# A diffusion layer's token-mixing heads with TensorE held to a written order

## The chip, the cores and the metric

One core of one Trainium2 chip runs the whole layer as one program. Its engines work in parallel, each on its own queue of instructions, and meet at semaphores: PE (TensorE, matrix products), DVE (VectorE), ACT (ScalarE), POOL (GpSimd) and SP, which issues DMAs. The metric is the device time of one execution in microseconds (us), as the median of several runs; one further execution was profiled.

## The reference

The layer has two parts. Token mixing computes eight heads over 256 context and 1024 latent tokens, four with an mLSTM memory and four with retention, each scanned in both directions in chunks of 128 tokens. Then a router lets each of 16 experts choose 128 tokens. Cut to what matters:

```python
def step(carry, inp):                      # mLSTM, one chunk, one direction
    ...
    s = jnp.einsum('bhtk,bhsk->bhts', qc, kc) * d_w
    num = jnp.einsum('bhts,bhsv->bhtv', s, vc) + i_w[..., None] * jnp.einsum('bhvk,bhtk->bhtv', C, qc)
    h = num / jnp.maximum(jnp.abs(den), jnp.exp(-m_t))[..., None]
    ...
y_m = jax.nn.sigmoid(parts[3]) * head_rmsnorm(m_sum, mlstm_norm_w)   # gate, norm per head
y_r = jax.nn.silu(parts[8]) * head_rmsnorm(r_sum, ret_norm_w)
y = jnp.concatenate([y_m, y_r], axis=-1) @ w_out
...
xl = xl + g2 * expert_choice_ffn(...)      # 16 experts, SwiGLU of width 2816
```

## The kernel before

The program has stages: adaLN and normalization of the inputs (to about 45 us), the heads, the output projection with the router, and the experts, which take two thirds of the time.

The heads run in the order 4, 0, 1, 2, 3, 5, 6, 7 (`HEADS`; 0 to 3 are mLSTM, 4 to 7 retention), called places 0 to 7 here. A head works through ten blocks of 128 tokens, two of context and eight latent ones. `gemm` (line 371) multiplies a block's normalized input with the head's 512 weight columns (gate, q, k, v): 24 products of 512 columns into the PSUM tile `g`, in eight steps of three, since inputs and weights are split in a high and a low part. A context block needs 256 columns only. `prep` (line 516) takes `g` apart: `v`, a gate `th` and `o`, and `qk` (with a rotary step for retention), transposes q and k (PSUM tile `T`, lines 570 and 571, copies `kT` and `qT`), forms the masked product `S` into `k1` or `k2`, and the state update `U` from `kw` and `v`, which a scan over the blocks takes into `st`.

`outp` (line 632) belongs to the head before: for one of its blocks the products `O` and `I` (for retention both in one tile) give the unnormalized rows; then `it`, `dn`, `hb`, `hs` divide and sum the two directions, `sq` and `rsqrt_mean` (lines 130 and 131, on POOL) give the norm `r`, line 674 multiplies to `z`, line 676 transposes `z` on TensorE, and a copy `zt` is stored. It is called after `prep` at the first eight blocks of the next head.

Weights of the next head come by `load_w`, four tiles `raw` of 512 KB, each split by ACT (`whi`, line 194) and DVE (`wlo`, line 195). The pool keeps eleven `whi` and eleven `wlo`, eight of the present head and three of the next. `ada2` (line 691) multiplies 512 KB of the adaLN matrix with a row, on DVE (line 694), at every second block. It shares the two buffers named `raw` with the weights.

Nothing fixes the order of TensorE in the heads: a scheduler puts each engine's instructions in an order by its own estimate of times. Each engine's queue is then worked in that order. An engine wrapped in `Ordered` (lines 138 to 144) keeps the order in which the code calls it; it is used before the heads only.

Of the kernel before, what the change touches and what calls it, by code (L numbers as in the profile page):

```python
# [8 lines left out]
F32 = mybir.dt.float32  # L9
# [12 lines left out]
NT = T // 128  # L22
# [98 lines left out]
def build(tc, A, out):  # L121
# [246 lines left out]

    pg_cur = [None]

    def gemm(wc, tt):
        his, los = wc
        c0 = 256 if tt < NTC else 0
        if tt != 1:
            pg_cur[0] = pg.tile([128, 512], F32, name="g")
        p = pg_cur[0]
        dst = p[:, 256 * tt:256 * tt + 256] if c0 else p
        hh, hl = htile(tt)
        for k in range(KD):
            for q, (a, w) in enumerate(((hh, his[k]), (hh, los[k]), (hl, his[k]))):  # L380
                PE.matmul(dst, lhsT=a[:, k], rhs=w[:, c0:512],  # L381
                          start=(k == 0 and q == 0), stop=(k == 7 and q == 2))
        return dst
# [132 lines left out]
    def prep(h, tt, p):  # L516
# [2 lines left out]
        lat = tt >= NTC  # L519
        NV = 130 if mls else 128  # L520
        r0, r1 = (row_of(0, tt, h), row_of(1, tt, h)) if mls else (0, 0)
        v = mp.tile([128, 130], F32, name="v", bufs=11)
        S.copy(v[:, 0:128], p[:, -128:])
        if mls:
            G.memset(v[:, 128:129], 1.0)
# [2 lines left out]
        if lat:  # L528
            th = mp.tile([128, 128], F32, name="th")
            S.activation(th, p[:, 0:128], AF.Tanh, scale=0.5)  # L530
            o = mp.tile([128, 128], F32, name="o", bufs=10)
            if mls:
                G.tensor_scalar(th, th, 0.5, 0.5, op0=ALU.mult, op1=ALU.add)
                G.tensor_tensor(o, th, d["nw"], op=ALU.mult)
            else:
                V.scalar_tensor_tensor(th, th, 1.0, p[:, 0:128], op0=ALU.add, op1=ALU.mult)
                G.tensor_scalar(th, th, 0.5, 1.0, op0=ALU.mult, op1=ALU.mult)
                G.tensor_tensor(o, th, d["nw"], op=ALU.mult)
            d["o"][tt] = o
# [23 lines left out]
        for dr in range(2):  # L563
            wcol = ct[:, 3, (r0, r1)[dr]:(r0, r1)[dr] + 1] if mls else d["kw"][:, dr:dr + 1]
            if tt == (NTT - 1, NTC)[dr]:
                continue
            G.tensor_scalar(kw[:, dr], qk[:, 1], wcol, QK, op0=ALU.mult, op1=ALU.mult)
        if lat:
            pt = ps.tile([128, 2, 128], F32, name="T", bufs=2)
            PE.transpose(pt[:, 0], qk[:, 0], ident)  # L570
            PE.transpose(pt[:, 1], qk[:, 1], ident)
            kT = mp.tile([128, 128], F32, name="kT")
            S.copy(kT, pt[:, 1])
            qT = mp.tile([128, 128], F32, name="k2", bufs=10) if mls else mp.tile([128, 128], F32, name="qTt")
            V.tensor_copy(qT, pt[:, 0])
            if not mls:
                qE = mp.tile([128, 2, 128], F32, name="k1", bufs=10)
                V.tensor_tensor(qE, pt[:, 0:1].broadcast_to([128, 2, 128]), d["e2"], op=ALU.mult)
                d["k1"][tt] = qE
            pS = psu.tile([128, 1, 128], F32, name="S")  # L580
            PE.matmul(pS[:, 0], lhsT=kT, rhs=qT, start=True, stop=True)
            if mls:
                mb = mp.tile([128, 2, 128], F32, name="t1")
                G.tensor_tensor(mb, aux, mbig, op=ALU.add)
                for dr in range(2):
                    r_ = (r0, r1)[dr]
                    S.activation(mb[:, dr], mb[:, dr], AF.Exp, bias=ct[:, 0, r_:r_ + 1], scale=-1.0)
                P = mp.tile([128, 2, 128], F32, name="k1", bufs=10)
                V.scalar_tensor_tensor(P, pS.broadcast_to([128, 2, 128]), QK, mb, op0=ALU.mult, op1=ALU.mult)
                d["k1"][tt], d["k2"][tt] = P, qT  # L590
            else:
                P = mp.tile([128, 128], F32, name="k2", bufs=10)
                V.scalar_tensor_tensor(P, pS[:, 0], QK, d["dm"], op0=ALU.mult, op1=ALU.mult)
                d["k2"][tt] = P
# [26 lines left out]
        else:  # L621
            if tt < NTT - 1:
                V.scalar_tensor_tensor(st(tt + 1)[:, 0], st(tt)[:, 0], decay(0), pU[:, 0], op0=ALU.mult, op1=ALU.add)
            if tt > NTC:
                if tt < NTT - 1:
                    S.copy(st(tt - 1)[:, 1], pU[:, 1])
                else:
                    V.scalar_tensor_tensor(st(tt - 1)[:, 1], st(tt)[:, 1], decay(1), pU[:, 1],
                                           op0=ALU.mult, op1=ALU.add)
        d["kt"][tt] = decay(1)  # L630

    def outp(h, tt, store=True):
        d = hd[h]
        mls = h < 4
        st = d["st"]
        if NTC < tt < NTT - 1:
            V.scalar_tensor_tensor(st[tt - 1][:, 1], st[tt][:, 1], d["kt"][tt], st[tt - 1][:, 1],
                                   op0=ALU.mult, op1=ALU.add)
        v, o, k1, k2 = d["v"][tt], d["o"][tt], d["k1"][tt], d["k2"][tt]
        hs = mp.tile([128, 128], F32, name="hs", bufs=3)  # L640
        sq = mp.tile([128, 128], F32, name="sq")
        ss = mp.tile([128, 1], F32, name="ss", bufs=3)
        if mls:
            r0, r1 = row_of(0, tt, h), row_of(1, tt, h)
            pO = ps.tile([128, 2, 130], F32, name="O")
            for dr in range(2):
                PE.matmul(pO[:, dr], lhsT=k1[:, dr], rhs=v, start=True, stop=True)
            pI = ps.tile([128, 2, 130], F32, name="I")
            PE.matmul(pI, lhsT=k2, rhs=st[tt], start=True, stop=True)
            it = mp.tile([128, 2, 130], F32, name="it")  # L650
            for dr in range(2):
                r_ = (r0, r1)[dr]
                S.activation(it[:, dr], pI[:, dr], AF.Copy, scale=ct[:, 1, r_:r_ + 1])
            V.tensor_tensor(it, pO, it, op=ALU.add)
            dn = mp.tile([128, 2], F32, name="dn")
            den = it[:, :, 128]
            V.tensor_tensor(dn, den, ct[:, 2, r0:r1 + 1:r1 - r0], op=ALU.max)
            V.scalar_tensor_tensor(dn, den, -1.0, dn, op0=ALU.mult, op1=ALU.max)
            V.reciprocal(dn, dn)
            hb = mp.tile([128, 128], F32, name="hb")  # L660
            G.tensor_scalar(hb, it[:, 1, 0:128], dn[:, 1:2], 1.0, op0=ALU.mult, op1=ALU.mult)
            V.scalar_tensor_tensor(hs, it[:, 0, 0:128], dn[:, 0:1], hb, op0=ALU.mult, op1=ALU.add)
            S.activation(sq, hs, AF.Square, accum_out=ss)
        else:
            pO = ps.tile([128, 128], F32, name="OI"[tt % 2])
            PE.matmul(pO, lhsT=k2, rhs=v[:, 0:128], start=True, stop=False)
            PE.matmul(pO, lhsT=k1[:, 0], rhs=st[tt][:, 0], start=False, stop=False)
            PE.matmul(pO, lhsT=k1[:, 1], rhs=st[tt][:, 1], start=False, stop=True)
            V.tensor_copy(hs, pO)
            S.activation(sq, hs, AF.Square, accum_out=ss)  # L670
        r = mp.tile([128, 1], F32, name="r", bufs=3)
        rsqrt_mean(r, ss, DH, mp)
        z = mp.tile([128, 128], F32, name="z")
        V.scalar_tensor_tensor(z, hs, r, o, op0=ALU.mult, op1=ALU.mult)
        pz = ps.tile([128, 128], F32, name="T", bufs=2)
        PE.transpose(pz, z, ident)
        zt = mp.tile([128, 128], F32, name="zt", bufs=3)
        S.copy(zt, pz)
        c = tt - NTC
        if store:  # L680
            nc.sync.dma_start(zt_d[h, :, c * 128:(c + 1) * 128], zt)
        return zt
# [58 lines left out]
        zsplit(c, 0, zr)  # L741

    todo = list(range(32))
    for n, h in enumerate(HEADS):
        head_start(h)
        for i in range(NTT):
            pr = ExitStack()
            if n == 0 and i < 4:
                pr.enter_context(tc.high_priority(offset=300))
            if i == 0:  # L750
                ps01 = [gemm(wcur, j) for j in range(NTC)]
            p = gemm(wcur, i) if i >= NTC else ps01[i]
            if n == 0 and i == 3:
                gates()
            if i == (6 if n == 0 else 0) and n + 1 < H:
                wnext = load_w(HEADS[n + 1])
            prep(h, i, p)
            pr.close()
            if n and i < NT:
                outp(HEADS[n - 1], NTT - 1 - i)  # L760
            if n == 1 and i == 0:
                silu_row()
            if n and i % 2 and todo:
# [1 line left out]
            if n == H - 1 and i == 4:  # L765
                V.tensor_tensor(mcol, mcol, cols[:, 16:48], op=ALU.add)
                V.scalar_tensor_tensor(mcol[:, 16:24], mcol[:, 16:24], 1.0, cols[:, 56:64], op0=ALU.add, op1=ALU.mult)
                g1bc.append(cp.tile([128, D], F32, name="crow"))
                col2row(g1bc[0], 0, lambda half: ps.tile([128, 512], F32, name="T", bufs=2))
            if n == H - 1 and i in (4, 5):  # L770
                zfirst(NT + 3 - i)
            if n == H - 1 and 5 < i < NTT:
                split_wout(*load_wout(0, 2 * (i - 6)))
            if n == H - 1 and i == 3:
                wo1 = [load_wout(1, k, 1) for k in range(6)]
        wcur = wnext

    def ygemm(y, c, half, ks):
        zh, zl = zz[0][:, c % 2], zz[1][:, c % 2]
# [611 lines left out]
```

## Time and profile before

| | us |
|---|---|
| median of 3 runs | 2279.93 (2277.79 to 2281.03) |
| the profiled execution, its own time | 2278.13 |
| its span, first to last instruction | 2276.4 |
| heads with output work beside them | 132 to 598 |
| experts | 772 to the end |

The profile gives for each engine the time it was busy, for each stretch the clock that TensorE was granted (1.00 is 2.4 GHz, 0.50 is 1.2 GHz), and for each wait the instruction that ended it. Long products overlap in the record: each lasts 0.39 us but the next starts 0.23 us later, so that the distance of two starts is the time one costs. Weight loads (PEld) run beside the products.

### The profile page before, as it was taken

How to read it: one execution, taken by the hardware profiler on the slowest of the kernel's cores; microseconds unless marked ns; L12 is line 12 of the kernel's file. 1: busy time of each engine (PE TensorE's matmuls, PEld its weight loads, DVE VectorE, ACT ScalarE, POOL GpSimd, SP SyncE). 2: the span in 40 equal slices, each digit the busy share in tenths (PEclk: the TensorE clock that was granted, in tenths of full speed). 3: DMA queues.
4: the chain of work that ended last, by engine and by line, in shares of the span. 5: the costliest groups of instructions: out<-in, count | busy, mean ns of one | idle time of the engine just before them, and what ended most of it. 6: DMA issues, size and time to landing. Idle time of an engine off the chain costs nothing.

```text
span 2276.4 us, 31305 instructions
## 1 busy us (share of the span) xinstructions
PE 2218.7 (97%) x11334; PEld 1852.1 (81%) x11334; DVE 1792.6 (79%) x2162; ACT 1431.2 (63%) x1854; POOL 355.1 (16%) x716
## 2 busy tenths in 40 slices
PE   7999999999899999999999999999999999999997
PEld 4788888888787788888888888888888888888885
DVE  6454545655735999999898898998988989889887
ACT  6533444322433676777777777677777777777775
POOL 2344444444411000000000000000000000000015
PEclk9999999999999999999999999999999999999999
DMA  7223322334375799999999999999999999999995
GB/s 279 64 61 107 102 69 77 103 111 125 106 242 204 308 357 370 355 389 390 372 395 365 380 392 367 401 366 382 389 368 400 367 382 389 368 391 377 371 405 233
DMA packets 134576, 664.71 MB, mean 292 GB/s; under 512 B 14381, under 2 KB 44181, under 8 KB 66837
## 3 DMA queue, kind: packets, MB, share of 16 engines
q1 hardware_dynamic: 127221, 634.73, 72.7%
q0 software_dynamic: 6768, 24.83, 3.7%
q10 hardware_dynamic: 432, 3.15, 0.4%
q8 instruction: 89, 1.46, 0.3%
q14 instruction: 66, 0.54, 0.1%
HBM read 637.50 MB, written 25.15 MB: 291 GB/s over the span
## 4 chain that ended last, share of the span: by engine, by line
PE 80%; DMA 7%; DVE 6%; issue 2%; ACT 2%; POOL 2%; SPq 0%; POOLq 0%; DVEq 0%; ACTq 0%
PE w_gate L144 20%; PE w_up L144 20%; PE y L144 19%; PE g L381 11%; DMA raw<-in_wada 4%; PE T L144 3%; PE y L783 2%; DVE lo L144 2%; DMA raw<-in_win 1%; PE U L599 1%; POOL r L131 1%; DMA xt<-in_x 1%; DVE raw L694 1%; DMA zr<-zt_d 1%; POOL rs_m L130 1%
## 5 line engine op out<-in xcount | busy, mean ns | idle before, releaser
L144 DVE TENSOR_TENSOR lo<-raw,hi 128x2048 fp32r<-128x2048 f32 x528 | 1180.0, 2285 | 74.8 <-ACT hi L144 70.2
L144 ACT CAST hi<-raw 128x2048 fp32r<-128x2048 f32 x528 | 979.6, 1904 | 41.5 <-PE w_up L144 38.6
L144 PE MATMUL w_gate<-hi,xh 128*128 128x512 f32 (+1 forms) x768 | 294.0, 383 | 0.7 <-ACT xh L144 0.7
L144 PE MATMUL w_gate<-hi,xl 128*128 128x512 f32 (+1 forms) x768 | 286.4, 373 | 0.0
L144 PE MATMUL w_up<-lo,xh 128*128 128x512 f32 (+1 forms) x768 | 285.4, 372 | 1.0 <-DVE lo L144 1.0
L144 PE MATMUL w_up<-hi,xh 128*128 128x512 f32 (+1 forms) x768 | 285.9, 372 | 0.0
L144 PE MATMUL w_gate<-lo,xh 128*128 128x512 f32 (+1 forms) x768 | 285.8, 372 | 0.0
L144 PE MATMUL w_up<-hi,xl 128*128 128x512 f32 (+1 forms) x768 | 285.3, 371 | 0.0
L144 ACT CAST th<-T 128x512 fp32r<-128x512 f32 x96 | 53.0, 552 | 340.7 <-PE T L144 340.7
L381 PE MATMUL g<-whi,hh 128*128 128x512 f32 (+1 forms) x640 | 246.6, 385 | 1.3 <-ACT qk L561 1.2
L381 PE MATMUL g<-whi,hl 128*128 128x512 f32 (+1 forms) x640 | 244.3, 382 | 1.0 <-DVE hl L361 1.0
L381 PE MATMUL g<-wlo,hh 128*128 128x512 f32 (+1 forms) x640 | 242.9, 380 | 0.0
L144 PE MATMUL y<-lo,th 128*128 128x512 f32 x704 | 222.3, 390 | 1.3 <-DVE lo L144 1.3
L144 PE MATMUL y<-hi,th 128*128 128x512 f32 x704 | 222.9, 390 | 0.5 <-ACT th L144 0.5
L144 PE MATMUL y<-hi,tl 128*128 128x512 f32 x704 | 222.3, 390 | 0.0
L144 PEld LDWEIGHTS w_up<-lo,xh 128*128 128x128 f32 x768 | 144.7, 188 | 26.2 <-DVE lo L144 1.6
L144 PEld LDWEIGHTS w_gate<-hi,xl 128*128 128x128 f32 x768 | 144.6, 188 | 26.0 <-DVE xl L144 0.2
L144 PEld LDWEIGHTS w_up<-hi,xl 128*128 128x128 f32 x768 | 144.7, 188 | 25.0
L144 PEld LDWEIGHTS w_up<-hi,xh 128*128 128x128 f32 x768 | 144.7, 188 | 24.7
L144 PEld LDWEIGHTS w_gate<-hi,xh 128*128 128x128 f32 x768 | 144.8, 188 | 23.5 <-ACT xh L144 0.9
L144 PEld LDWEIGHTS w_gate<-lo,xh 128*128 128x128 f32 x768 | 145.0, 189 | 23.1
L1284 POOL DMA_INDIRECT acc_d<-yo,idx x15 | 23.8, 1587 | 874.8 <-DVE yo L144 874.8
(376 smaller groups left out, 3214.0 us busy)
## 6 DMA issues: line engine op xcount, KB each, us to landing
raw<-in_w_down SPq DMA_DIRECT2D x176, 1024.0 KB, 7.5
raw<-in_w_up SPq DMA_DIRECT2D x175, 1024.0 KB, 7.3
raw<-in_w_gate SPq DMA_DIRECT2D x174, 1024.0 KB, 7.6
raw<-in_wada SPq DMA_DIRECT2D x32, 512.0 KB, 4.3
raw<-in_win SPq DMA_DIRECT2D x28, 512.0 KB, 3.9
wa<-in_wada SPq DMA_DIRECT2D x16, 512.0 KB, 6.7
xt<-in_x SPq DMA_DIRECT2D x16, 512.0 KB, 7.8
aux<-in_k_rope SPq DMA_DIRECT2D x32, 128.0 KB, 2.1
```

The costliest lines, as they stand in the source:

```text
L130: G.tensor_scalar(m, ss, 1.0 / n, EPS, op0=ALU.mult, op1=ALU.add)
L131: G.tensor_tensor(dst, m, mhalf, op=ALU.pow)
L144: return lambda *a, **k: tc.keep_in_program_order(f(*a, **k))
L381: PE.matmul(dst, lhsT=a[:, k], rhs=w[:, c0:512], start=(k == 0 and q == 0), stop=(k == 7 and q == 2))
L599: PE.matmul(pU[:, dr], lhsT=kw[:, dr], rhs=v[:, 0:NV], start=True, stop=True)
L694: V.scalar_tensor_tensor(raw, raw, 1.0, crow, op0=ALU.mult, op1=ALU.mult, accum_out=mcol[:, n:n + 1])
L783: PE.matmul(y, lhsT=a[:, k], rhs=w[:, k], start=(k == 0 and q == 0), stop=(k == 7 and q == 2))
L1284: nc.gpsimd.indirect_dma_start(out=acc_d, out_offset=bass.IndirectOffsetOnAxis(ap=idx[:, :1], axis=0), in_=yo, in_offset=None, compute_op= ...
```

## The change

In places 1 to 7 TensorE keeps the order of the code. `prep` becomes a generator with three stops, and its short products are called from the next block's `gemm`: the transpositions of q and k in the middle of it (`between`, at step 4 of 8), `S` and `U` behind it (`behind_gemm`). `outp` is cut in two. `outp_rows`, up to `z`, follows behind the product of each latent block, now at blocks 2 to 9; `outp_turn`, which transposes and stores `z`, comes in the middle of the next product. For the first latent block the two context blocks' remaining steps go into the middle of its product. `v` and `o` get one buffer more, `hs` one less, and `zfirst` comes one block later in the last head. Head 0 and what follows the heads are left to the scheduler.

```diff
-    def gemm(wc, tt):
+    def gemm(wc, tt, mid=None):
...
         for k in range(KD):
+            if mid and k == KD // 2:
+                mid()
...
-        v = mp.tile([128, 130], F32, name="v", bufs=11)
+        v = mp.tile([128, 130], F32, name="v", bufs=12)
...
-            o = mp.tile([128, 128], F32, name="o", bufs=10)
+            o = mp.tile([128, 128], F32, name="o", bufs=11)
...
             G.tensor_scalar(kw[:, dr], qk[:, 1], wcol, QK, op0=ALU.mult, op1=ALU.mult)
+        yield
         if lat:
             pt = ps.tile([128, 2, 128], F32, name="T", bufs=2)
...
+        yield
+        if lat:
             pS = psu.tile([128, 1, 128], F32, name="S")
...
         d["kt"][tt] = decay(1)
+        yield
 
     def outp(h, tt, store=True):
+        z, = outp_rows(h, tt)
+        return outp_turn(h, tt, z, store)
+
+    def outp_rows(h, tt):
...
-        hs = mp.tile([128, 128], F32, name="hs", bufs=3)
+        hs = mp.tile([128, 128], F32, name="hs", bufs=2)
...
         V.scalar_tensor_tensor(z, hs, r, o, op0=ALU.mult, op1=ALU.mult)
+        return z,
+
+    def outp_turn(h, tt, z, store=True):
         pz = ps.tile([128, 128], F32, name="T", bufs=2)
         PE.transpose(pz, z, ident)
...
+    parts, turns = [], []
+
+    def between():
+        if parts:
+            next(parts[0])
+        if turns:
+            outp_turn(*turns.pop(0))
+
+    def behind_gemm(n, tt):
+        while parts:
+            next(parts.pop(0))
+        if n and tt >= NTC:
+            o = NTT + 1 - tt
+            turns.append((HEADS[n - 1], o) + outp_rows(HEADS[n - 1], o))
+
+    PE_free, PE_fixed = PE, Ordered(PE)
     for n, h in enumerate(HEADS):
         head_start(h)
+        PE = PE_fixed if n else PE_free
         for i in range(NTT):
...
+            elif i == 0:
+                ps01 = [gemm(wcur, 0)]
+                between()
+                ps01.append(gemm(wcur, 1))
+                behind_gemm(n, 0)
+                p = ps01[0]
+            elif i == 1:
+                p = ps01[1]
+            elif i == NTC:
+                def first_two():
+                    next(parts[0])
+                    next(parts.pop(0))
+                    if turns:
+                        outp_turn(*turns.pop(0))
+                    next(parts[0])
+                p = gemm(wcur, i, first_two)
+                behind_gemm(n, i)
+            else:
+                p = gemm(wcur, i, between)
+                behind_gemm(n, i)
...
-            prep(h, i, p)
+            g_ = prep(h, i, p)
+            if n == 0:
+                for _ in g_:
+                    pass
+            else:
+                next(g_)
+                parts.append(g_)
             pr.close()
-            if n and i < NT:
-                outp(HEADS[n - 1], NTT - 1 - i)
```

TensorE in the middle of an mLSTM head, with an mLSTM head's output beside it. `g` is the long product, `T<-ident,qk` the transposition of q and k, `T<-ident,z` that of the finished rows. Before, as the scheduler put it:

```order
L381 MATMUL g<-whi,hh_77 128x512
L599 MATMUL U<-v,kw 128x130 x2
L647 MATMUL O<-v,k_2037 128x130 x2
L649 MATMUL I<-st,k_1943 128x260
L381 MATMUL g<-wlo,hh_77 128x512
...
L581 MATMUL S<-k_2506,kT 128x128
...
L676 MATMUL T<-ident,z 128x128
L570 MATMUL T<-ident,qk 128x128
L571 MATMUL T<-ident,qk 128x128
```

With the change, one block, with twelve products `g` at each line of dots (every instruction called through `Ordered` bears the line of that wrapper, 144):

```order
L144 MATMUL S<-k_3361,kT 128x128
L144 MATMUL U<-v,kw 128x130
L144 MATMUL O<-v,k_3078 128x130 x2
L144 MATMUL I<-st,k_3053 128x260
...
L144 MATMUL T<-ident,qk 128x128 x2
L144 MATMUL T<-ident,z 128x128
...
L144 MATMUL S<-k_3456,kT 128x128
```

The short products were spread in places that the scheduler chose block by block; now they stand in two groups, and the transposition of `z` stands twelve products behind the `I` of the same rows.

VectorE at the end of place 2, where the next head's weights are split (`wlo`) and `ada2` runs (`raw,mcol`). Before:

```order
L674 SCALAR_TENSOR_TENSOR z<-hs,r,o 128x128
...
L195 TENSOR_TENSOR wlo<-raw,whi 128x512 x3
L589 SCALAR_TENSOR_TENSOR k_2988<-S,t_2984 128x256
...
L195 TENSOR_TENSOR wlo<-raw,whi 128x512 x2
L694 SCALAR_TENSOR_TENSOR raw,mcol<-raw,crow 128x1024
L589 SCALAR_TENSOR_TENSOR k_3084<-S,t_3080 128x256
L694 SCALAR_TENSOR_TENSOR raw,mcol<-raw,crow 128x1024
```

With the change:

```order
L707 SCALAR_TENSOR_TENSOR raw,mcol<-raw,crow 128x1024
L195 TENSOR_TENSOR wlo<-raw,whi 128x512
L594 SCALAR_TENSOR_TENSOR k_3078<-S,t_3074 128x256
L628 SCALAR_TENSOR_TENSOR st<-st,dec,U 128x130
L707 SCALAR_TENSOR_TENSOR raw,mcol<-raw,crow 128x1024
L664 TENSOR_TENSOR it<-O,it 128x260
L707 SCALAR_TENSOR_TENSOR raw,mcol<-raw,crow 128x1024
...
L707 SCALAR_TENSOR_TENSOR raw,mcol<-raw,crow 128x1024
L672 SCALAR_TENSOR_TENSOR hs<-it,dn,hb 128x128
L707 SCALAR_TENSOR_TENSOR raw,mcol<-raw,crow 128x1024
L684 SCALAR_TENSOR_TENSOR z<-hs,r,o 128x128
```

Before, the last `z` of a head's output stood ahead of this run of loads; now the last block's `it`, `hs` and `z` stand among them, `z` behind five of the `ada2` products here and behind four at the end of place 3.

## Rows read from the trace of the kernel before

**Rows 1.** The page, part 1: busy time, share of the span, instructions.
```profile
PE 2218.7 (97%) x11334; PEld 1852.1 (81%) x11334; DVE 1792.6 (79%) x2162; ACT 1431.2 (63%) x1854; POOL 355.1 (16%) x716
```
**Rows 2.** Busy time by stage; stretch, length, engines, TensorE's clock, DMA share, GB/s.
```profile
132.00:598.00 466.00, 458.30 (x2564) 392.99 (x2563) 253.42 (x729) 169.17 (x634) 210.13 (x519) 1.00 0.32 97
...
772.00:2276.00 1504.00, 1488.35 (x7351) 1243.67 (x7349) 1355.82 (x905) 1107.90 (x893) 74.88 (x51) 1.00 0.96 374
```
**Rows 3.** What TensorE waited for, 132 to 598 us: total, times, longest.
```profile
PE T L676 <- DVE z L674: 1.6, 2, 1.4
```
**Rows 4.** Timeline of TensorE, 229 to 233 us: start, length, instruction.
```profile
229.51 0.27 PE L570 MATMUL T<-ident,qk 128*128 128x128 f32 x1
229.62 0.27 PE L571 MATMUL T<-ident,qk 128*128 128x128 f32 x1
...
230.66 0.39 PE L381 MATMUL g<-whi,hh 128*128 128x512 f32 x1
230.89 0.61 PE L599 MATMUL U<-v,kw 128*128 128x130 f32 x4
231.34 0.61 PE L647 MATMUL O<-v,k 128*128 128x130 f32 x4
231.78 0.60 PE L649 MATMUL I<-st,k 128*128 128x260 f32 x2
232.03 0.58 PE L381 MATMUL g<-wlo,hh 128*128 128x512 f32 x1
232.45 0.39 PE L381 MATMUL g<-whi,hl 128*128 128x512 f32 x1
```
**Rows 5.** Timelines of TensorE, ScalarE and VectorE from 319 us, one output block.
```profile
319.24 0.60 PE L649 MATMUL I<-st,k 128*128 128x260 f32 x2
```
```profile
319.88 0.63 ACT L653 ACTIVATE it<-I,ct 128x130 f32<-128x130 f32 x2 [0.17 <-PE I L649]
...
320.55 0.43 DVE L654 TENSOR_TENSOR it<-O,it 128x260 f32<-128x260 f32 x1 [2.45 <-ACT it L653]
...
324.92 0.35 DVE L674 SCALAR_TENSOR_TENSOR z<-hs,r,o 128x128 f32<-128x128 f32 x1
```
**Rows 6.** Timeline of all engines from 372 us: one block's chain to z.
```profile
372.88 0.43 DVE L654 TENSOR_TENSOR it<-O,it 128x260 f32<-128x260 f32 x1
...
374.04 0.37 POOL L661 TENSOR_SCALAR hb<-it,dn 128x128 f32<-128x128 f32 x1
...
375.66 0.55 POOL L131 TENSOR_TENSOR r<-rs_m,mhalf 128x1 f32<-128x1 f32 x1
...
376.24 0.35 DVE L674 SCALAR_TENSOR_TENSOR z<-hs,r,o 128x128 f32<-128x128 f32 x1 [1.44 <-POOL r L131]
```
**Rows 7.** Groups by line, 132 to 598 us: busy, mean ns, idle before.
```profile
L567 POOL TENSOR_SCALAR kw<-qk,kw 128x128 f32<-128x128 f32 x54 | 30.3, 562 | 13.7 <-ACT qk L561 7.7 <-PE U L599 0.8 <-ACT kT L573 0.5
...
L559 POOL TENSOR_TENSOR qk<-t,t 128x256 f32<-128x256 f32 x24 | 20.1, 838 | 5.0 <-DVE t L558 2.2 <-PE T L571 1.7 <-PE g L381 0.9
```
**Rows 8.** Timeline of VectorE at the end of place 2.
```profile
260.96 2.24 DVE L195 TENSOR_TENSOR wlo<-raw,whi 128x512 fp32r<-128x512 f32 x3 [2.12 <-ACT whi L194]
...
276.97 1.23 DVE L694 SCALAR_TENSOR_TENSOR raw<-raw,crow 128x1024 f32<-128x1024 f32 x1
```
**Rows 9.** Busy time by short stretches, columns as in rows 2.
```profile
36.00:40.00 4.00, 1.29 (x9) 0.96 (x8) 3.89 (x9) 3.68 (x7) 0.00 (x0) 1.00 0.98 393
40.00:44.00 4.00, 1.67 (x8) 1.43 (x8) 2.99 (x7) 3.90 (x8) 2.38 (x3) 0.57 1.02 411
44.00:51.00 7.00, 5.97 (x27) 5.32 (x26) 6.46 (x12) 5.83 (x14) 5.41 (x8) 0.52 0.61 224
612.00:616.00 4.00, 1.69 (x12) 1.19 (x11) 2.33 (x6) 1.05 (x1) 0.00 (x0) 1.00 0.96 380
```
**Rows 10.** The page, part 6: DMA issues, KB each, median us to landing.
```profile
raw<-in_wada SPq DMA_DIRECT2D x32, 512.0 KB, 4.3
```

More of the change, by code (lines that the diff above doesn't have):

```diff
@@ L749, in build @@
                 pr.enter_context(tc.high_priority(offset=300))
-            if i == 0:
-                ps01 = [gemm(wcur, j) for j in range(NTC)]
-            p = gemm(wcur, i) if i >= NTC else ps01[i]
+            if n == 0:
+                if i == 0:
+                    ps01 = [gemm(wcur, j) for j in range(NTC)]
+                p = gemm(wcur, i) if i >= NTC else ps01[i]
+            elif i == 0:
[18 more added lines that the diff above has]
+                behind_gemm(n, i)
             if n == 0 and i == 3:
@@ L756, in build @@
                 wnext = load_w(HEADS[n + 1])
-            prep(h, i, p)
+            g_ = prep(h, i, p)
+            if n == 0:
+                for _ in g_:
[3 more added lines that the diff above has]
+                parts.append(g_)
             pr.close()
-            if n and i < NT:
-                outp(HEADS[n - 1], NTT - 1 - i)
             if n == 1 and i == 0:
@@ L768, in build @@
                 g1bc.append(cp.tile([128, D], F32, name="crow"))
+                PE = PE_free
                 col2row(g1bc[0], 0, lambda half: ps.tile([128, 512], F32, name="T", bufs=2))
-            if n == H - 1 and i in (4, 5):
-                zfirst(NT + 3 - i)
+                PE = PE_fixed
+            if n == H - 1 and i in (5, 6):
+                zfirst(NT + 4 - i)
             if n == H - 1 and 5 < i < NTT:
@@ L776, in build @@
         wcur = wnext
+    PE = PE_free
+    for g_ in parts:
+        for _ in g_:
+            pass
+    parts.clear()
+    while turns:
+        outp_turn(*turns.pop(0))
     def ygemm(y, c, half, ks):
```

## The prediction

> **What bounds the kernel now.** I read the engines' busy shares first. TensorE (PE) is busy for 97% of the span [rows 1], so time can only come from its idle time, its switching, or from waits that are added to it. The busy time by stage comes next. The stretch in which seven heads run beside each other's output work, 132 to 598 us, holds 458.30 us of TensorE in 466.00; the expert stage after 772 us is denser still, at full clock, and the change does not touch it [rows 2]. What the heads can give back is therefore small: 7.7 us of idle time, and the cost of changing between long and short products. The table of who waited for whom shows why the idle time is so small: TensorE waited only 1.6 us in all for a `z`, in 2 of 56 cases [rows 3]. The scheduler had put the transposition of `z` behind its input nearly everywhere.
>
> **What TensorE does for a block.** A long product (`g`) takes a slot of 0.23 us (230.66 to 230.89), a pair of `U` 0.45, a pair of `O` 0.44, an `I` 0.25 until the next starts, a transposition 0.11 [rows 4]. A latent block is 24 long products, 5.5 us, and some 1.7 us of short ones. Each return from short to long costs extra: from 230.66 to 232.45 there are two long slots (0.46) and shorts of 1.14, and 0.19 is left over. I take 0.1 as the price of an interruption, with 0 and 0.19 as ends.
>
> **What is saved.** From the two orders I count some 193 interruptions of the long products in heads 1 to 7 before and 124 after; 69 x 0.1 is 7 us. With all 7.7 us of idle time the change could give back 15 us at most in this stretch. The buffers that it resizes (`v`, `o` one more, `hs` one less) move no work: `hs` is read some 2 us after it is written, while a block lasts 7. Head 0 and the closing stages are free as before; I put them at nothing, within 5 us either way, by the 1.3 us waits that such stretches show.
>
> **What is added: the wait for z.** The fixed order puts twelve long products and two transpositions between a block's `I` (or `O`) and the transposition of its `z`. I take the room from rows 4. `I` starts at 231.78 and ends at 232.38. The next long products start at 232.03 and 232.45, ten more at 0.23 each, two transpositions at 0.11: the slot of `z` comes at 235.20, which is 2.82 us after the end of `I`.
> The work in between is a chain over three engines. From the end of `I` (319.84) ScalarE makes two `it` and VectorE starts its addition at 320.55: 0.71 us [rows 5]. From that addition, through three small `dn`, `hb` on POOL, `hs`, a square on ScalarE, `rs_m` and `r` on POOL, to the end of `z` it is 372.88 to 376.59, so 3.71 us, with almost nothing in the way [rows 6]. Together 4.42 us against 2.82: TensorE stands for 1.6 us. Nothing passes it, because TensorE's queue is now held to the written order; behind `z` wait twelve long products, then `S` and `U` of the same block. On a busier tile the chain was longer: 5.43 us from the end of `I` to the end of `z` at 325.27 [rows 5], a wait of 2.6. I take 1.6, since the changed order leaves little between the steps, and keep 2.6 as the upper end. The lower end is 1.6 too, since rows 6 show the chain nearly bare.
>
> Now by head. In the places 2 to 4 an mLSTM head prepares while an mLSTM head is output: the first 7 rows of each cost 1.6, so 21 x 1.6 = 34 us. The seventh row has two weight subtractions of 0.75 us (three take 2.24 [rows 8]) put ahead of `hs` on VectorE; so has the one in place 5: 4 x 1.5 = 6. In place 5 a retention head prepares, and `hb` queues on POOL behind the rotary sum (0.838) and two `kw` (0.562 each) [rows 7]: 1.96 us that can start about 0.5 after `I` ends (an estimate, from the five VectorE products ahead), while `dn` is ready 0.71 + 1.16 after it; `hb` is some 0.7 late, the wait 2.3, 7 x 2.3 = 16. In places 6 and 7 both heads are retention: the chain is only `hs`, square, `rs_m`, `r`, `z`, but `r` stands behind the rotary sum and both `kw` on POOL: 0.9 + 0.84 + 1.12 + 0.55 + 0.5 = 3.9 against 2.8, a wait of 1.1, 15 times: 17. In place 1 (a retention head's output beside an mLSTM head) POOL holds the shorter `kw` and no rotary sum: an estimate of 0.4, a third of that, x 7 = 3. Sum: 76 us. If the retention waits vanish it is 56.
>
> **What is added: the end of a head.** The 512 KB tiles for the next head's weights and for the adaLN products share two buffers, so VectorE gets them one transfer apart, 4.3 us each [rows 10]. Before, the first weight subtraction of such a run starts at 260.96 and the fourth adaLN product ends at 278.20: 17.2 us [rows 8], and no `z` stands among them; the next one comes after the run. Now the last block's `z` stands behind four or five of these products, as the order of VectorE shows. Its transposition is wanted 13.3 us after that block's product begins (two halves of 2.8, the seventh row's wait and transpositions of 3.2, shorts 1.4, the context block 2.9, two transpositions 0.2). The run starts 2.4 us in, so `z` is ready at 2.4 + 17.2 + 0.4 = 20.0: a wait of 6.7. Since the last weight subtraction now also stands behind the first adaLN product, it may be 11.8. I take 8 for the four heads 2 to 5, so 32 us, and 4 each for the ends of heads 1 and 6, whose `z` has one or two such products ahead: 8. The lower end is 0, if the loads come earlier than before.
>
> **The clock.** From 36 to 44 us TensorE was busy for only 2.96 of 8 us; it then ran at the lower level, 1.2 GHz (a clock of 0.57 and 0.52 over 11 us, 5.97 us of work in the last 7, half of that lost) [rows 9]. Between 612 and 616 us it was busy for only 1.69 of 4 us and kept 2.4 GHz. So I charge the four long waits with 2 us each (ends 0 and 4), and the short ones with nothing: 8 us.
> The Trainium skill speaks against the change here: its page "TensorE: Matmul & The Clock Gate", section "A second HAM failure mode: psum-queue depth-cycling", says that frequent small idle times between groups of products can make the clock swing between its levels. By that rule the 1.6 us waits would cost clock as well; the 612 to 616 row does not bear it out, and I carry it as a rival.
>
> **Sum.** 76 + 6 + 32 + 8 + 8 - 15; the 6 of the seventh rows is in the 76, so it is 76 + 32 + 8 + 8 - 15 = 109 us. The profiled execution took 2278.13 us (span 2276.4); 2278.1 + 109 = 2387. The median of the runs is 1.8 us above the profiled one, which I neglect.
>
> **The rivals.** *No wait for z (faster).* If `z` were ready in its slot everywhere, only the saving is left: 2278 - 15 = 2263. For it speaks that TensorE waited for `z` only twice before; against it that the slot is now 2.82 us behind, and the bare chain 4.42. It decides from a chain below 2.8 us. *Waits inside heads only.* If the loads at a head's end come early enough that `z` does not stand behind them, the ends and their clock go: 76 - 15 = 61, 2339. *The clock swings.* If every short wait brings 1.2 GHz for about half of the blocks, a block's 7.2 us of TensorE become 14.4 and its wait goes, some 5.6 us more for half of 54 blocks: 150 more, about 2540. *The order is not what it says*: the built order shows it on every block, so no chance.
>
> **How the numbers follow.** The forecast (both kinds of wait, 2340 to 2447) has 0.75, waits inside heads only 0.15, the clock 0.05, no wait 0.05. Low end: the mLSTM waits alone, 32 x 1.6 - 15 = 36, so 2314. High end: 32 x 2.6 = 83, retention 20, ends 4 x 11.8 + 12 = 59, clock 16, less 10: 168, so 2446. What a measurement can tell from no change is about 0.2%, 4.6 us. Faster by more has 0.04 of the last rival's 0.05, the same 0.01, slower 0.95.
>
> **What would show it.** In the profile after, the table of waits should have TensorE's transposition of `z` waiting for VectorE near the top, some 50 times, 1.6 us typically and 7 us or more four times, each of these behind an adaLN product that waits for its transfer; the seven heads should take some 570 us instead of 466; the expert stage should keep its length. I am wrong if `z` waits are few, if its chain measures below 3 us, if the long waits are for something else, or if the granted clock is at 0.5 inside the heads.

## The result and the profile after

| | before | after |
|---|---|---|
| median of 4 runs, us | 2278.86 (2277.13 to 2281.03) | 2431.32 (2430.11 to 2432.48) |
| profiled execution, span | 2276.4 | 2428.2 |

The changed kernel takes 1.0668 times as long (95% interval 1.065 to 1.0687), 152 us more. The forecast was 2387 with a range of 2314 to 2446: the direction and the wait for `z` held, the middle is 44 us short. The page of the changed kernel, part 1, answers to [rows 1]:

```profile
PE 2256.9 (93%) x11334; PEld 1874.6 (77%) x11334; DVE 1798.2 (74%) x2162; ACT 1435.3 (59%) x1854; POOL 348.1 (14%) x716
```

The same 11334 products now fill 93% of a longer span. The busy time by stage (columns as in [rows 2]) says which stage grew; the first row is heads 1 to 7, from the first product of head 1 to the last `g` of head 7, the second the expert stage:

```profile
141.10:751.70 610.60, 494.97 (x2560) 415.94 (x2560) 257.57 (x721) 170.74 (x622) 202.83 (x512) 0.94 0.25 74
902.00:2424.00 1522.00, 1510.65 (x7450) 1261.95 (x7450) 1375.83 (x922) 1125.57 (x908) 70.94 (x51) 1.00 0.96 374
```

The expert stage is as dense as it was. The seven heads take 610.6 us, cut at the same products 465.9 before. TensorE stands idle there for 115.6 us instead of 7.7, is busy for 495.0 instead of 458.2, and has a mean clock of 0.94 instead of 1.00. What it waited for (heads 0 to 7; total, times, longest) answers to [rows 3]:

```profile
PE T L144 <- DVE z L684: 109.0, 49, 9.4
PE T L144 <- POOL qk L561: 6.0, 3, 2.5
PE S L586 <- DVE k L598: 3.6, 1, 3.6
```

`z` went from 2 waits to 49. One block's chain, from the timeline of all engines in place 3 (start, length, instruction, idle time before it and what ended that), reads as [rows 5] and [rows 6] did:

```profile
340.43 0.60 PE L144 MATMUL I<-st,k 128*128 128x260 f32 x2
341.13 0.63 ACT L663 ACTIVATE it<-I,ct 128x130 f32<-128x130 f32 x2 [0.29 <-PE I L144]
...
343.12 0.37 POOL L671 TENSOR_SCALAR hb<-it,dn 128x128 f32<-128x128 f32 x1 [0.58 <-DVE dn L669]
...
345.31 0.35 DVE L684 SCALAR_TENSOR_TENSOR z<-hs,r,o 128x128 f32<-128x128 f32 x1 [0.47 <-POOL r L131]
...
345.72 0.33 PE L144 MATMUL T<-ident,z 128*128 128x128 f32 x1 [1.71 <-DVE z L684]
```

`I` ends at 341.03, `z` at 345.66: a chain of 4.63 us, each engine idle ahead of its link, so nothing else is in its way. TensorE came to the slot at 344.01 (345.72 less 1.71), 2.98 us behind `I`, and stood 1.71. The table by place (TensorE alone: stretch, length, busy, clock, DMA share, GB/s) shows where the rest lies; the first row is head 0, the others places 1 to 7:

```profile
44.70:141.10 96.40, 86.46 (x441) 0.89 0.25 75
141.10:208.10 67.00, 65.57 (x361) 0.98 0.13 38
208.10:298.60 90.50, 72.99 (x367) 0.92 0.27 78
298.60:388.20 89.60, 69.29 (x367) 0.94 0.23 71
388.20:477.10 88.90, 69.30 (x365) 0.96 0.24 72
477.10:575.60 98.50, 73.20 (x366) 0.90 0.24 74
575.60:658.00 82.40, 69.27 (x367) 0.94 0.25 72
658.00:751.70 93.70, 75.35 (x381) 0.93 0.32 101
```

Before, these took 87.8, 65.2, 68.1, 67.2, 67.6, 66.5, 65.2 and 66.1 us. The idle time of a place is its length less its busy time: 17.5 to 25.3 us in places 2 to 5.

The long waits stand in the first block of a place, where the last `z` of the place before is still due. From VectorE's timeline at the start of place 3, with the product that waits:

```profile
300.97 1.23 DVE L707 SCALAR_TENSOR_TENSOR raw<-raw,crow 128x1024 f32<-128x1024 f32 x1 [2.49 <-DMA raw<-in_wada]
302.12 0.42 DVE L664 TENSOR_TENSOR it<-O,it 128x260 f32<-128x260 f32 x1
302.46 1.22 DVE L707 SCALAR_TENSOR_TENSOR raw<-raw,crow 128x1024 f32<-128x1024 f32 x1
...
305.67 1.23 DVE L707 SCALAR_TENSOR_TENSOR raw<-raw,crow 128x1024 f32<-128x1024 f32 x1 [1.33 <-DMA raw<-in_wada]
306.82 0.35 DVE L672 SCALAR_TENSOR_TENSOR hs<-it,dn,hb 128x128 f32<-128x128 f32 x1
308.39 1.23 DVE L707 SCALAR_TENSOR_TENSOR raw<-raw,crow 128x1024 f32<-128x1024 f32 x1 [1.22 <-DMA raw<-in_wada]
309.55 0.35 DVE L684 SCALAR_TENSOR_TENSOR z<-hs,r,o 128x128 f32<-128x128 f32 x1
```
```profile
301.45 0.28 PE L144 MATMUL g<-wlo,hh 128*128 128x256 f32 x1
301.57 0.28 PE L144 MATMUL g<-whi,hl 128*128 128x256 f32 x1
...
309.95 0.47 PE L144 MATMUL T<-ident,z 128*128 128x128 f32 x1 [7.88 <-DVE z L684]
...
311.08 0.41 PE L144 MATMUL g<-wlo,hh 128*128 128x256 f32 x1
311.29 0.41 PE L144 MATMUL g<-whi,hl 128*128 128x256 f32 x1
```

Four adaLN products (L707) stand between or ahead of the links `it`, `hs` and `z` of one chain, and three of them wait for their transfer first (5.04 us in all, beside 1.2 us of work for each of the four). The first blocks of places 4, 5 and 6 have such waits of 7.08, 9.44 and 6.75 us. What the clock did around this one, by short stretches (columns as in [rows 2]):

```profile
302.00:309.95 7.95, 0.07 (x2) 0.00 (x1) 5.27 (x15) 0.67 (x3) 1.25 (x7) 0.64 0.64 199
309.95:314.40 4.45, 4.45 (x21) 4.45 (x22) 1.29 (x2) 1.58 (x4) 0.00 (x0) 0.50 0.53 154
314.40:323.00 8.60, 8.60 (x50) 7.51 (x49) 5.11 (x13) 2.75 (x11) 3.05 (x10) 1.00 0.26 75
```

It fell during the wait, and the first 4.45 us of work behind it ran at 1.2 GHz (0.50): the same half-width products start 0.21 us apart there and 0.12 us apart ahead of the wait, so nearly half of that time is lost. In heads 1 to 7 the clock fell 14 times, before not once. Laid over TensorE's instructions, the clock's records put 58.8 us of the heads' work at the lower level (2.7 of them behind a fall at the end of head 0), so 29.4 us are lost to it if half is taken, and some 26 by those distances.

### The profile page after: what moved, and what is told of

Read it like the earlier page. It is cut to its first block, busy times and chain, and to the rows that moved or that the text cites. A ratio compares the mean times of both kernels' runs of the same rounds, so it can differ in the third digit from the quotient of the medians.

```text
span 2428.2 us, 31289 instructions
## 1 busy us (share of the span) xinstructions
PE 2256.9 (93%) x11334; PEld 1874.6 (77%) x11334; DVE 1798.2 (74%) x2162; ACT 1435.3 (59%) x1854; POOL 348.1 (14%) x716
## 4 chain that ended last, share of the span: by engine, by line
PE 75%; DVE 8%; issue 5%; DMA 5%; POOL 4%; ACT 2%; SPq 0%; POOLq 0%; ACTq 0%; DVEq 0%
PE w_gate L144 19%; PE w_up L144 19%; PE y L144 18%; PE g L144 7%; PE T L144 3%; PE y L847 2%; DMA raw<-in_wada 2%; DVE lo L144 2%; PE g L383 2%; POOL r L131 1%; DMA zr<-zt_d 1%; POOL kw L569 1%; POOL rs_m L130 1%; DMA xt<-in_x 1%; DVE z L684 1%
## 5 line engine op out<-in xcount | busy, mean ns | idle before, releaser
L144 PE MATMUL g<-whi,hh 128*128 128x512 f32 (+1 forms) x560 | 233.6, 417 | 0.0
L144 PE MATMUL g<-whi,hl 128*128 128x512 f32 (+1 forms) x560 | 218.0, 389 | 0.0
L144 PE MATMUL g<-wlo,hh 128*128 128x512 f32 (+1 forms) x560 | 217.4, 388 | 0.0
L144 PEld LDWEIGHTS y<-lo,th 128*128 128x128 f32 x704 | 132.0, 188 | 29.1 <-DVE lo L144 1.6
```

The source lines that it names most:

```text
L144: return lambda *a, **k: tc.keep_in_program_order(f(*a, **k))
```

## The experiments

All ratios are against the kernel before, on the same chip and in the same job; the changed kernel stands at 1.0668.

**Does z's slot make the waits?** e1_late moves the transposition of `z` from the middle of the next long product to its end.

```diff
     def between():
         if parts:
             next(parts[0])
-        if turns:
-            outp_turn(*turns.pop(0))
...
     def behind_gemm(n, tt):
         while parts:
             next(parts.pop(0))
+        if turns:
+            outp_turn(*turns.pop(0))
...
-                    if turns:
-                        outp_turn(*turns.pop(0))
```

> One edit: z of a block is transposed half a long product later, behind the block's S and U and ahead of the next rows, instead of in the middle of the next long product. Theory of the prediction (z's slot stands 2.82 us behind the end of I, the chain from I to z takes 4.4 us): the slot then stands some 6 us behind I, so the waits of T for z inside the heads (1.69 to 1.71 us a row in places 2 to 4, 1.9 to 2.1 in place 5, about 75 us of idle in all, by the gaps of the changed kernel) vanish, the waits at the ends of heads (6.8 to 9.4 us) lose 2 to 3 us each, and about half of the 30 us that the lower clock costs goes with them: 2431 - 65 - 15 = 2350 us, 2335 to 2370. Rival one (the fixed order itself costs, whichever input is late): another product of the chain, S, U or O, waits in z's place, and the time stays above 2400. Rival two (the waits inside heads also feed the ends): all of it goes, 2285 to 2300.

Measured: 2325.03 us, ratio 1.0213 (1.0196 to 1.0231), 10 us below the expected range. Its waits in heads 0 to 7:

```profile
PE T L144 <- DVE z L684: 21.4, 9, 7.1
PE T L144 <- POOL qk L561: 6.3, 3, 3.7
...
PE S L586 <- DVE k L598: 3.5, 1, 3.5
```

49 waits became 9, and two thirds of the loss are gone with one call moved. Other products took over little: `S` and `U`, which did not wait in heads 1 to 7 of the changed kernel, now wait some 8 us in four waits. That is against rival one. The work at the lower clock fell from 58.8 to 16.3 us, more than the half that was expected.

**Is the size of a wait what slot and chain leave?** e9_z_k6 moves the slot by six products only.

```diff
             if mid and k == KD // 2:
                 mid()
+            if mid and k == 6 and turns:
+                outp_turn(*turns.pop(0))
...
-        if turns:
-            outp_turn(*turns.pop(0))
...
```

> The changed kernel with z transposed six products later in the same long product, behind the 18th of its 24 instead of the 12th; T of q and k stays behind the 12th, and the start of a head is as it was. Theory of the prediction (a fixed slot against a chain of fixed length, so that the wait falls by as much as the slot moves): six products at 0.23 us are 1.4 us, so the waits of 1.7 us a row fall to 0.3, those of 2.5 to 1.1 and those of 1.9 to 0.5, some 27 rows x 1.4 + 5 x 1.4 + place 7's 5 = 50 us; the waits at the starts of heads stay; with 5 to 10 us of low clock: 2431 - 57 = about 2374 us, 2362 to 2388. Rival (the chain to z follows the long product, since VectorE and ScalarE are fed by it: z comes later too): row waits of 1 us or more, above 2400.

Measured: 2365.50 us, 1.0383 (1.0365 to 1.0401), inside the range. One block of it, from the timeline of all engines, and the transposition of the next row:

```profile
323.36 0.60 PE L144 MATMUL I<-st,k 128*128 128x260 f32 x2
...
328.25 0.35 DVE L686 SCALAR_TENSOR_TENSOR z<-hs,r,o 128x128 f32<-128x128 f32 x1 [0.47 <-POOL r L131]
...
328.66 0.33 PE L144 MATMUL T<-ident,z 128*128 128x128 f32 x1 [0.32 <-DVE z L686]
```
```profile
336.62 0.33 PE L144 MATMUL T<-ident,z 128*128 128x128 f32 x1 [0.33 <-DVE z L686]
```

From the end of `I` (323.96) to the end of `z` (328.60) it is 4.64 us, as in the changed kernel (4.63). The slot stands 4.38 behind `I` instead of 2.98, 1.40 later for six products of 0.23, and the wait fell from 1.71 to 0.32, by 1.39. The chain is fixed and does not follow the long product: slot and chain make the wait, to a few hundredths.

**How much is the wait for z, all told?** e2_ready transposes the block's `v`, which is long ready, in the same slots.

```diff
-            turns.append((HEADS[n - 1], o) + outp_rows(HEADS[n - 1], o))
+            outp_rows(HEADS[n - 1], o)
+            turns.append((HEADS[n - 1], o, hd[HEADS[n - 1]]["v"][o][:, 0:128]))
```

> The product in z's slot transposes the block's v, which is ready long before, instead of z; z is still computed, but its rows of the output are not (seven heads give v in place of z). Same products, same places, no wait for z. Theory of the prediction (nearly all of the loss is T's wait for z, and the clock that falls because of it): the 118 us of such waits and the 30 us of low clock go, the small waits for qk and k (some 10 us) stay: 2431 - 118 - 25 = about 2288 us, 2278 to 2305. Rival (VectorE and GpSimd are behind with everything, and T for z only comes first): the waits move to S, O and I behind it, and the time stays above 2350.

Measured: 2309.89 us, 1.0141 (1.0124 to 1.0158), 5 us above the theory's range and far below the rival's. So some 120 us of the 152, by the ratios, hang on the wait for `z`. Heads 1 to 7 of it, TensorE alone, and the waits that are left there:

```profile
141.20:630.50 489.30, 462.57 (x2554) 0.99 0.31 92
```
```profile
PE T L144 <- POOL qk L561: 6.4, 5, 2.0
PE U L144 <- DVE ub L620: 5.8, 4, 2.0
PE U L144 <- DVE st L633: 4.8, 2, 2.7
```

Of the 23 us that these heads still take above before, 19 are idle time, most of it in waits of short products near the starts of heads, where two products of half the width leave little room between the stages. `U` and `S` do not wait in heads 1 to 7 of the changed kernel, where TensorE comes to them later, behind its waits for `z`; this is what the expectation had left out. Without the 3.6 us that its 7.2 us of work at the lower clock cost, the busy time is 459.0, against 458.2 before: no saving of busy time by the fixed order shows.

**Which part of the change is it?** e5_free keeps everything but the fixed order.

```diff
-    PE_free, PE_fixed = PE, Ordered(PE)
+    PE_free = PE_fixed = PE
```

> One edit: the changed kernel with its code written in the new order (parts, turns, buffers as they are), but TensorE's products are not held in program order; the scheduler places them as it did before the change. Theory (the loss is the fixed order alone, the rest of the change is worth next to nothing): the short products move behind inputs that are ready, T waits little for z, and the time is within 1% of before, 2268 to 2295 us. Rival (rows and z are written half a block later, so VectorE's and GpSimd's work shifts too and the scheduler can't cover that): above 2310.

Measured: 2286.23 us, 1.0035 (1.0023 to 1.0048). TensorE in heads 1 to 7, and its wait for `z` in all heads:

```profile
133.00:606.40 473.40, 460.27 (x2558) 1.00 0.33 98
```
```profile
PE T L689 <- DVE z L684: 1.9, 3, 1.2
```

With the order free, 3 waits and no fall of the clock: the order is 144 us of the 152, and the rest of the change, code in parts and other buffers, costs 8 (idle 13.1 instead of 7.7, the others in busy time). Which of these it is was not taken apart.

**The ends of heads.** e3_adafirst brings the adaLN products of a place to its start.

```diff
-            if i == (6 if n == 0 else 0) and n + 1 < H:
+            if n and i == 1:
+                for _ in range(5):
+                    if todo:
+                        ada2(todo.pop(0))
+            if i == (6 if n == 0 else 1) and n + 1 < H:
                 wnext = load_w(HEADS[n + 1])
...
-            if n and i % 2 and todo:
-                ada2(todo.pop(0))
```

> One edit: the five adaLN products that a place of the head loop issues at blocks 1, 3, 5, 7 and 9 all stand at block 1, ahead of the next head's weight loads (which move from block 0 to block 1); z's slot is as in the changed kernel. Theory of the prediction (at the end of a head VectorE stands at an adaLN product that waits for its transfer behind the weights, with z queued behind it): the waits of 7.9, 7.1, 9.4 and 6.8 us at the ends fall to 1.5 to 3 us, about 22 us of idle, and 10 us of low clock go with them: about 2399 us, 2385 to 2412. Rival (five adaLN products in a row hold VectorE at the start of each head in the same way): waits of the same sum stand in the first blocks of a head, and the time is 2420 to 2445.

Measured: 2422.35 us, 1.0649 (1.0628 to 1.067), not clearly below the changed kernel's 1.0668 (1.065 to 1.0687). The theory failed, and the time lies in the rival's range: `z` still has 49 waits, 102.1 us instead of 109.0. VectorE in the first blocks of place 4 shows why:

```profile
394.58 1.22 DVE L707 SCALAR_TENSOR_TENSOR raw<-raw,crow 128x1024 f32<-128x1024 f32 x1 [1.54 <-DMA raw<-in_wada]
395.74 0.35 DVE L672 SCALAR_TENSOR_TENSOR hs<-it,dn,hb 128x128 f32<-128x128 f32 x1
...
397.12 1.23 DVE L707 SCALAR_TENSOR_TENSOR raw<-raw,crow 128x1024 f32<-128x1024 f32 x1 [1.03 <-DMA raw<-in_wada]
398.27 0.35 DVE L684 SCALAR_TENSOR_TENSOR z<-hs,r,o 128x128 f32<-128x128 f32 x1
```

The start of a place is where the last `z` of the place before is due, so the products stand between the same links as ever; the wait there was 8.07 us. That did not tell whether adaLN is the cause, so e7_noada takes these products away.

```diff
-            if n and i % 2 and todo:
-                ada2(todo.pop(0))
+            if n == 1 and i == 1:
+                V.memset(mcol, 0.0)
```

> The changed kernel without the adaLN products of the heads: neither their transfers nor VectorE's 32 products are issued, and their result is taken as zero (the output is wrong for that). z's slot is as in the changed kernel. Theory of the prediction (at the ends of the heads z is queued behind an adaLN product that waits for its transfer; moving these to the start of a head, e3_adafirst, only brought them to the same blocks): the waits of 7.9, 7.1, 9.4 and 6.8 us fall to 1.5 to 3, and with 10 us of low clock the time is about 2397 us, 2385 to 2405; the waits of 1.7 us a row stay. Rival (at the ends VectorE is late with the weights' splits or the new head's first blocks, and adaLN is only in that queue): the long waits keep over 5 us each, above 2415.

Measured: 2392.83 us, 1.05 (1.0478 to 1.0522), as the theory said. The first blocks of places 3 to 6:

```profile
300.70 0.33 PE L144 MATMUL T<-ident,z 128*128 128x128 f32 x1 [2.61 <-DVE z L684]
...
384.19 0.46 PE L144 MATMUL T<-ident,z 128*128 128x128 f32 x1 [2.16 <-DVE z L684]
...
468.60 0.33 PE L144 MATMUL T<-ident,z 128*128 128x128 f32 x1 [3.28 <-DVE z L684]
...
559.03 0.33 PE L144 MATMUL T<-ident,z 128*128 128x128 f32 x1 [2.15 <-DVE z L684]
```

The waits of 7.88, 7.08, 9.44 and 6.75 us are 2.61, 2.16, 3.28 and 2.15, while the rows keep their 1.7: the adaLN products are the cause of 21 of the 31 us in the long waits. This run takes away their transfers and VectorE's time for them together, so how much is due to the transfers alone is not shown by it.

**The clock.** e4_filler puts products that nobody reads into the waits.

```diff
-        pz = ps.tile([128, 128], F32, name="T", bufs=2)
+        pt = ps.tile([128, 512], F32, name="T", bufs=2)
+        pz = pt[:, 0:128]
+        for _ in range(fill[0]):
+            PE.matmul(pt[:, 128:512], lhsT=hT[1][0][:, 0, 0:128], rhs=wcur[0][0][:, 128:512], start=True, stop=True)
         PE.transpose(pz, z, ident)
...
+            fill[0] = (40 if 2 < n < 7 else 0) if i == 0 else (10 if 1 < n < 6 else 0)
```

> The waits are left as they are, but TensorE does idle products in them: ahead of z's transposition stand 10 extra products of 384 columns of operands that are long ready (some 1.6 us) in places 2 to 5, and 40 (some 6.5 us) in the first block of places 3 to 6; their results go to unused columns of T and are read by nobody. They prolong nothing where the wait is longer than they are. Theory (the falls of the granted clock follow from the waits and cost some 30 us of the heads): most of the 60 us of work at 1.2 GHz in places 2 to 5 runs at 2.4 GHz, 15 to 25 us less: about 2411 us, 2403 to 2418. Rival one (the clock falls for another reason, or the chain to z is what sets the pitch of a block and gives back nothing): 2428 to 2435. Rival two (the extra products delay what they should hide): above 2435.

Measured: 2415.97 us, 1.0607 (1.0589 to 1.0625): 440 products more, and 14 us less than the changed kernel by the ratios. Places 2 to 5 of it:

```profile
207.80:562.20 354.40, 339.63 (x1859) 1.00 0.25 74
```

and of the changed kernel:

```profile
208.10:575.60 367.50, 284.79 (x1459) 0.93 0.25 74
```

The clock stays at 2.4 GHz but for one short fall, and these places take 13 us less although the rows still come as far apart as before (9.36 us from one transposition of `z` to the next in both). Work at the lower clock there fell from 35.0 to 3.4 us; half of the difference is 15.8. So the clock's loss is real, and TensorE's idle time in the waits is its cause.

e10_filler_ends fills the first blocks of places 3 to 6 alone (`fill[0]` is 0 in the rows).

> As e4_filler, but with the extra products in the first block of places 3 to 6 alone (40 there), none in the rows of a head. Theory of the prediction (a fall of the clock belongs to a long wait, the row waits of 1.7 us cost no clock): the falls at the ends of places 2 to 5 go, four times 2.4 us, those that follow waits of 2.5 to 4.5 us stay: 2431 - 10 = 2421 us, 2418 to 2425. Rival one (the rows matter too: with the ends filled the clock falls behind row waits instead): 2426 to 2434. Rival two (the falls in the rows only follow on those at the ends): as e4_filler, 2413 to 2417.

Measured: 2435.57 us, 1.0693 (1.0673 to 1.0713). That is nearest to rival one. TensorE in places 3 and 4, and in place 5 with the start of place 6:

```profile
298.00:516.00 218.00, 182.54 (x1007) 1.00 0.25 78
516.00:595.00 79.00, 62.89 (x305) 0.89 0.26 77
```

In places 3 and 4 the clock no longer falls, behind rows that still wait 1.7 us each. In the rows of place 5, which wait 1.9 to 2.1, it falls three times (at 516.7, 537.2, 557.6) where the same rows of the changed kernel have one fall. The length of one wait does not settle it: a wait of 2.5 us at the end of place 2 is followed by a fall, those of 2.5 at the ends of places 3 and 4 are not. The time tells little here: two of the filled waits were followed by a new one of 2.2 to 2.3 us of `U` for `kw`, so the filling did not only fill, and what the clock gave back there can't be read from the time.

**Head 0, and a second step back.** e6_late_tail adds to e1_late that head 0's last block is spread over the next products, as in the other heads.

```diff
-            if n == 0:
+            if n == 0 and i < NTT - 1:
                 for _ in g_:
                     pass
```

> The kernel of e1_late with one more edit: the short products of the first head's last block are no longer all issued before the first long product of the next head, but at places in it, as in all other heads. In e1_late the first head takes 96.9 us instead of 87.9 of before: S waits 3.5 us for P, T 0.9 for qk, and 7 us of work run at the lower clock behind that. Theory: these 6 to 9 us go: 2325 - 7 = 2318 us, 2315 to 2320. Rival (the next head's first products need that long for their own inputs): no change, 2323 to 2327.

Measured: 2317.56 us, 1.0165 (1.0146 to 1.0184). Head 0 takes 89.1 us instead of 96.9, with some of its short products now in head 1, and heads 1 to 7 take 1.0 us more; the wait of `S` is 1.3 us instead of 3.5. That is as expected in the main. e8_late2_tail holds `z` for one more block:

```diff
-        if turns:
+        if len(turns) > 1:
             outp_turn(*turns.pop(0))
```

> The kernel of e6_late_tail with z's transposition a whole block later still (two z's are held; the order is otherwise the same). e1_late keeps 9 waits of T for z, 21 us in all, one of 7.1 us, at the starts of heads. Theory: they all go, as in e2_ready, where the seven heads took 489 us instead of 504 of e1_late: 2318 - 14 = 2304 us, 2298 to 2311; what is left above before are waits of S and U in the first blocks of heads (20 us). Rival (the rest of the chain shares VectorE's lateness at those places, so other products wait in z's place): 2313 to 2320.

Measured: 2312.30 us, 1.0145 (1.0126 to 1.0164), between the two expectations, and by the intervals not clearly below e6_late_tail. No wait of T for `z` is left, but T waits 12.5 us for `qk` (6 times) and `U` and `S` some 15 us more. This is the fastest version with a fixed order that computes the layer. None beats the kernel before, and the heads leave little to win: 7.7 us of idle time there.

## Why the prediction was right, and what it mis-sized

The bill, heads 1 to 7 from the tables above, term by term:

| term | predicted, us | measured, us |
|---|---|---|
| idle time of TensorE in heads 1 to 7: 76 + 32 + 8, less the 7.7 of before | +108 | +107.9 |
| clock in these heads, half of its work at the lower level | +8 | +29.4 |
| other busy time (interruptions saved) | -7 | +7.4 |
| head 0 | 0, within 5 | +8.6 |
| ahead of head 0 and behind the heads | 0 | -1.5 |
| sum of the span | 109 | 151.8 |

**The wait inside heads: right.** Slot 2.82 and chain 4.42 were forecast; they measured 2.98 and 4.63, and the wait of 1.6 came as 1.69 to 1.71. e9_z_k6 shows that the difference of the two is the mechanism, e1_late and e2_ready that it carries most of the loss. Place 5's 2.3 came as 1.86 to 2.11; the forecast's own terms there (0.5 + 1.96 against 0.71 + 1.16) leave 0.6, not 0.7, so 2.2. The step from rows of the kernel before held because the chain there was already nearly bare [rows 6].

**The retention places: right in sum, not apart.** 1.1 us a row was forecast for places 6 and 7. Place 6 has about 0.7: the rotary sum takes 0.74 us and a `kw` 0.46 there, where 0.838 and 0.562 were taken from [rows 7], means over several heads. Place 7 has 18.3 us of idle time where about 12.5 was forecast; 6.0 of it in three waits of T for `qk`, of which the prediction had none. Place 1 had 1.4 instead of 3. These errors cancel, and the match of the first line of the bill is in part luck.

**The ends of heads: right.** 8 us each, behind adaLN products that wait for their transfers; 7.88, 7.08, 9.44 and 6.75 came, and e7_noada shows that the adaLN products make two thirds of them. The 8 was picked between 6.7 and 11.8, and the 11.8 has no working, so that the mean of 7.8 comes so near is in part luck. The 4 us at the ends of heads 1 and 6 came as 3.07 and 3.63.

**The clock: the term that failed.** The price of one long wait was near (2 us taken, 2.2 to 2.7 measured), the number of falls was not: 14 instead of 4. "The short ones with nothing" was read from one stretch, 612 to 616 us in [rows 9]. The trace of before already held a sign of the contrary a little later: behind waits of 2.31 us (to 615.47) and 1.26 us (to 626.06) the clock fell, as the stretch from 628 us shows (columns as in [rows 2]).

```profile
628.00:632.00 4.00, 4.00 (x14) 3.16 (x15) 0.17 (x1) 0.39 (x2) 0.00 (x0) 0.62 0.18 49
```

In the heads, waits come back in every block, and ten falls stand behind waits of 1.9 to 4.5 us; e7_noada, without any wait over 5 us there, has ten falls too. A clock of 0.5 inside the heads was one of the forecast's own signs of being wrong, and for this term it came true. The row waits of 1.7 us alone brought none: places 3 and 4 of e10_filler_ends have ten of them, and one of 2.5 each, at full clock. The Trainium skill's rule that was set against the change (page "TensorE: Matmul & The Clock Gate", section "A second HAM failure mode: psum-queue depth-cycling": frequent small idle times between groups of products make the clock swing) is borne out by the trace in part: ten falls behind the shorter waits, but none behind those ten rows of 1.7 us. The rival made of it, every second block at half clock and 150 us, was far too dear.

**The interruptions: no saving.** e2_ready has the changed kernel's order without the wait for `z`, and its busy time less the clock's loss is 459.0 against 458.2. The price of 0.1 us an interruption was a remainder of one pair of slots in [rows 4], and 0 was its lower end. In the changed kernel the busy time grew by 7.4 us beyond the clock; with 52 stops of over 0.25 us in the heads that would be 0.14 a stop, an estimate, if all of it goes to starting again. No run measured it by itself. By the same estimate the 19 stops of e2_ready, against 7 before, may hide some 2 us of saving, not the 7 that were forecast.

**Head 0: outside its bounds.** I took it as free as before. But the first fixed product of head 1 comes behind all of head 0's short products, and its last block's chain, with `S` waiting 3.6 us for VectorE's line 598, lies open. e6_late_tail, built on e1_late, gave some 7 us of this back (all eight heads together).

**The rivals.** No wait for `z` fell at once: 49 waits. Waits inside heads only fell with the long waits at the ends. The clock's swing was real at a fifth of its price.

## What to carry to other kernels

Before fixing the order of an engine, measure for each moved product the chain that makes its input, from the end of the product that starts it, and place the slot behind the longest form of that chain; here half a block more (in e1_late the slot stands 6.26 us behind the end of `I` instead of 2.98) was worth some 104 us by the ratios. At the borders, where another stream (transfers, a new head) shares the engine that makes the input, the chain is longer than in the rows, and a fixed order cannot step around it. On TensorE price a wait that comes back every block higher than its idle time: the clock took 29 us on top of 108.

## What the hardware showed that was not expected

The clock fell not only at the long waits. In e10_filler_ends, where those of places 3 and 4 are filled, it stayed at 2.4 GHz in these two places, whose rows wait 1.7 us, and fell three times in the rows of place 5, which wait 1.9 to 2.1; in the changed kernel ten of 14 falls stand behind waits under 5 us. What besides the length of a wait decides about a fall stays open. And work that nobody reads can pay: 440 extra products in e4_filler kept places 2 to 5 at 2.4 GHz but for one short fall and made the kernel 14 us faster. Some 69 fewer returns from short to long products saved no busy time that shows (459.0 us in e2_ready against 458.2), although the trace of before has a remainder of 0.19 us at one of them [rows 4].
